# One layer's rotation angles move from VectorE to GpSimd in a two-layer hybrid block

## The chip, the cores and the metric

The kernel runs on one core of a Trainium2 chip, in one launch. The metric is the device time of that launch in microseconds (us). Engines are named as the profile names them: PE is TensorE (matmuls), DVE is VectorE, ACT is ScalarE, POOL is GpSimd, SP is SyncE (which issues the DMAs).

## The reference, cut to what matters

Two layers are applied to x (256 tokens x 1024 channels, float32). Each layer normalises x, multiplies it by one wide input matrix, feeds the columns of the product to three mixers (an attention, a gated linear attention called GLA, and a diagonal state-space scan called S5), gates and adds the three results, and ends in a feed-forward block with 4096 hidden units. The part that the change touches is the S5 mixer:

```
lam = complex(min(lam_re, -1e-4), lam_im)
step = exp(log_dt)
lam_bar = exp(lam * step)                       # 32 groups x 64 states
bu = einsum(u, b_bar)                           # complex input of each state
states = scan(s[t] = lam_bar * s[t-1] + bu[t])  # over the tokens
y = real(einsum(states, c)) + d * u
```

The kernel doesn't scan complex numbers. With lam_bar = r * exp(i * theta) it turns the input by -theta * t, scans the real and the imaginary part with the real factor r, and turns the result back. For that it needs sin and cos of theta * t for every state and every step. It works on pairs of tokens, so t runs over 128 steps, and 2048 states lie as 128 partitions x 16: two tables of 128 x 2048 per layer, `sinT` and `cosT`.

## The kernel before, in words

**Matmuls.** Each float32 product is made of three matmuls of rounded parts (lines 182 to 186, `mm3`): high x high, high x low, low x high. Weights are streamed from memory in chunks of 128 x 1024. For each chunk SP issues a DMA into `raw`, ACT rounds it to `hi` (line 164), and DVE computes `lo` = raw - hi (line 165). There are 3 `raw` buffers and 4 pairs `hi`, `lo`; a chunk is prepared 3 chunks before the one in use (`AHEAD`, lines 168 to 180). The order of the chunks is fixed when the program is built.

**Order.** The mixers of a layer are cut into steps, and the order of the steps is written out by hand in the strings `STEPS` (lines 153 to 167); a number behind a step moves its priority. A scheduler then lays out each engine's instruction list from these priorities and from what it takes to be ready. On the chip every engine works through its own list in order. An instruction whose input is late holds up everything behind it on that engine, even when that is ready.

**S5 constants.** `s5_pre` (line 319) makes the constants of the S5 mixer from the layer's parameters. It is a generator: each `P` in the first string of `STEPS` runs it to its next `yield`. For layer 0 it runs among the mixers' own steps. For layer 1 it runs during layer 0's feed-forward block (lines 1245 to 1254). It makes, in this order: the decay and the angle theta of each state (`thi` and `tlo` are the high and low part of theta / pi, lines 343 to 350); the matrices `bbar` and `cmat` (complex products on DVE in `z1` to `z4`, lines 390 to 399, spread by ACT, line 403); the transposes `Btp` of `bbar` on PE (line 438); a small matrix `K0`; then the angles.

**The angles.** Lines 456 to 474 treat four groups `ph` of 128 x 512 (four columns of states by 128 steps). For each group DVE multiplies the step number `iota` by `thi` (line 464, one instruction with both inputs broadcast), rounds to a whole turn by adding and subtracting a large constant (line 466, into the memory of `cosT`), subtracts that (line 467), adds `iota` x `tlo` (line 470, four instructions of 128 x 128), and takes off whole turns again (lines 472 and 473). ACT then makes sin, half-angle sin and its square (lines 478 to 480), and DVE turns the square into cos (line 484). The first reader of the tables is `s5_r`, lines 594 to 612, on DVE.

**POOL before.** POOL sets memory to constants (lines 270, 282, 289, 408, 409, 450, 922) and copies the decay `r2` into the scan's factor `R`, once per S5 row (line 589).

Of the kernel before, what the change touches and what calls it, by code (L numbers as in the profile page):

```python
# [14 lines left out]
ALU = mybir.AluOpType  # L15
# [71 lines left out]
class Kern:  # L87
# [231 lines left out]
    def s5_pre(self, l):  # L319
        nc, v, tt = self.nc, self.nc.vector, self.nc.vector.tensor_tensor  # L320
# [22 lines left out]
        thi = self.tiny.tile([128, n], F32R, tag="s5thi", name="thi", bufs=1)  # L343
        v.tensor_scalar(out=thi, in0=th, scalar1=1.0 / math.pi, scalar2=None, op0=ALU.mult)
        thi = thi.bitcast(F32)
        tlo = tn("tlo")
# [85 lines left out]
        for i in range(4):  # L432
# [3 lines left out]
            for q in range(4):  # L436
                c = (4 * i + q) * 128
# [6 lines left out]
        for q in range(4):  # L444
            for r in range(4):
                i = q * 4 + r
# [6 lines left out]
        s["K0"] = K0  # L453
        yield

        phs = [self.s2(f"Q{4 + i}", "ph") for i in range(4)]
        sinT, cosT = self.b8(1, "sinT"), self.b8(0, "cosT")
        kk = cosT
        for i in range(4):
            c = slice(512 * i, 512 * i + 512)  # L460
            ph = phs[i]
            ph3 = ph.rearrange("p (s c) -> p s c", s=4)
            b3 = [128, 4, 128]
            tt(out=ph3, in0=self.iota.unsqueeze(1).to_broadcast(b3),
               in1=thi[:, 4 * i:4 * i + 4].unsqueeze(2).to_broadcast(b3), op=ALU.mult)
            v.tensor_scalar(out=kk[:, c], in0=ph, scalar1=RND, scalar2=RND, op0=ALU.add, op1=ALU.subtract)
            tt(out=ph, in0=ph, in1=kk[:, c], op=ALU.subtract)
            yield
            for j in range(4):
                v.scalar_tensor_tensor(out=ph3[:, j], in0=self.iota, scalar=tlo[:, 4 * i + j:4 * i + j + 1],  # L470
                                       in1=ph3[:, j], op0=ALU.mult, op1=ALU.add)
            v.tensor_scalar(out=kk[:, c], in0=ph, scalar1=RND, scalar2=RND, op0=ALU.add, op1=ALU.subtract)
            tt(out=ph, in0=ph, in1=kk[:, c], op=ALU.subtract)
            yield
        for i in range(4):
            c = slice(512 * i, 512 * i + 512)
            ph = phs[i]
# [4 lines left out]
        for i in range(4):  # L482
            c = slice(512 * i, 512 * i + 512)
# [880 lines left out]
```

## Time and profile before

| | |
|---|---|
| median of 3 runs | 887.69 us (887.6 to 888.2) |
| the profiled execution's own time | 888.1 us |
| its span, first to last instruction | 886.3 us |
| PE busy | 866.6 us, 98% of the span |
| DVE busy | 672.6 us, 76% |
| ACT busy | 518.9 us, 59% |
| POOL busy | 22.5 us, 3% |
| granted TensorE clock, mean | 0.998 |

The span is what the trace covers; the execution's own time is 1.8 us more. Matmuls are pipelined and a matmul's end is modelled, so that a PE which is shown as busy is not proof that it lost nothing; a stretch in which PE is not shown as busy is time lost. Other engines' shares are shares of the whole span and hide that the stages differ: layer 0's mixers run from some 20 to 200 us, its feed-forward block follows.

### The profile page before, as it was taken

The numbers are of one execution on the slowest core, as the hardware profiler recorded it, in microseconds if no ns is written. First come the engines' busy times: TensorE is split into PE (matmuls) and PEld (weight loads), VectorE is DVE, ScalarE is ACT, GpSimd is POOL, SyncE is SP. The second block draws the span as 40 slices with busy tenths as digits, with TensorE's granted clock in tenths as the row PEclk, the third lists the DMA queues.
The fourth block names the chain that finished last, engine by engine and source line by source line (L and its number), as shares of the span: only waits on it lengthen the run. The fifth ranks groups of instructions, "written<-read, shape, count | busy, mean of one in ns | idle before, by whom it ended". The sixth has DMA issues, their size and how long they took to land.

```text
span 886.3 us, 16190 instructions
## 1 busy us (share of the span) xinstructions
PE 866.6 (98%) x6412; PEld 798.4 (90%) x6412; DVE 672.6 (76%) x1283; ACT 518.9 (59%) x794; POOL 22.5 (3%) x35
## 2 busy tenths in 40 slices
PE   7999999999999999999999999999999999999998
PEld 6879988899989999999988989898999899999996
DVE  7999999987767975885576887899877765555554
ACT  6877887654456565664457647874544554444441
POOL 2000000010000000000000000002000000000000
PEclk9999999999999999999999999999999999999999
DMA  7534434246664665666645644344555566656552
GB/s 259 181 122 148 153 119 145 72 153 189 190 197 159 193 192 168 190 188 190 190 143 167 184 150 150 96 143 141 170 167 167 190 187 191 185 186 184 188 190 92
DMA packets 42267, 147.79 MB, mean 167 GB/s; under 512 B 4688, under 2 KB 5328, under 8 KB 42192
## 3 DMA queue, kind: packets, MB, share of 16 engines
q1 hardware_dynamic: 42192, 146.76, 53.0%
q8 instruction: 50, 0.82, 0.4%
q14 instruction: 25, 0.20, 0.1%
HBM read 145.70 MB, written 1.05 MB: 166 GB/s over the span
## 4 chain that ended last, share of the span: by engine, by line
PE 81%; DVE 12%; ACT 3%; issue 2%; DMA 2%; SPq 0%; DVEq 0%; ACTq 0%
PE fp L184 7%; PE fp L186 7%; PE fp L185 7%; PE fo L184 7%; PE fo L185 7%; PE fo L186 7%; DVE lo L165 4%; PE gp L184 3%; PE gp L185 3%; PE gp L186 2%; PE brp L184 2%; PE brp L186 2%; PE brp L185 2%; PE wo L186 2%; PE wo L184 2%
## 5 line engine op out<-in xcount | busy, mean ns | idle before, releaser
L165 DVE TENSOR_TENSOR lo<-raw,hi 128x1024 fp32r<-128x1024 f32 (+2 forms) x276 | 332.8, 1207 | 157.7 <-ACT hi L164 156.9
L164 ACT CAST hi<-raw 128x1024 fp32r<-128x1024 f32 (+2 forms) x276 | 285.9, 1037 | 278.4 <-PE fp L185 78.9
L184 PE MATMUL fp<-h,hi 128*128 128x256 f32 x512 | 145.2, 284 | 0.0
L185 PE MATMUL fp<-h,hi 128*128 128x256 f32 x512 | 145.0, 283 | 0.0
L186 PE MATMUL fp<-h,lo 128*128 128x256 f32 x512 | 144.9, 283 | 0.0
L184 PE MATMUL gp<-h,hi 128*128 128x256 f32 x384 | 109.8, 291 | 1.0 <-ACT ppt L858 0.8
L186 PE MATMUL gp<-h,lo 128*128 128x256 f32 x384 | 107.6, 286 | 0.0
L185 PE MATMUL gp<-h,hi 128*128 128x256 f32 x384 | 107.2, 285 | 0.0
L184 PE MATMUL fo<-hi,r 128*128 128x512 f32 x256 | 100.1, 391 | 0.0
L185 PE MATMUL fo<-lo,r 128*128 128x512 f32 x256 | 99.9, 390 | 0.0
L186 PE MATMUL fo<-hi,r 128*128 128x512 f32 x256 | 99.6, 389 | 0.0
L184 PEld LDWEIGHTS fp<-h,hi 128*128 128x128 f32 x512 | 98.1, 192 | 0.9
L185 PEld LDWEIGHTS fp<-h,hi 128*128 128x128 f32 x512 | 98.2, 192 | 0.9
L186 PEld LDWEIGHTS fp<-h,lo 128*128 128x128 f32 x512 | 98.2, 192 | 0.0
L184 PEld LDWEIGHTS gp<-h,hi 128*128 128x128 f32 x384 | 72.7, 192 | 3.0 <-ACT ppt L858 1.0
L185 PEld LDWEIGHTS gp<-h,hi 128*128 128x128 f32 x384 | 72.5, 191 | 1.0 <-issue 0.5
L186 PEld LDWEIGHTS gp<-h,lo 128*128 128x128 f32 x384 | 72.6, 191 | 0.1
L186 PEld LDWEIGHTS fo<-hi,r 128*128 128x128 f32 x256 | 48.1, 188 | 10.2
L184 PEld LDWEIGHTS fo<-hi,r 128*128 128x128 f32 x256 | 48.2, 188 | 9.2
L185 PEld LDWEIGHTS fo<-lo,r 128*128 128x128 f32 x256 | 48.2, 188 | 8.9
L1054 ACT ACTIVATE gt<-gt,hgateb 128x256 f32<-128x256 f32 x48 | 21.9, 501 | 9.3 <-DVE gt L1051 9.1
L184 PE MATMUL wo<-hi,mh 128*128 128x512 f32 x64 | 24.9, 395 | 0.0
(397 smaller groups left out, 1778.5 us busy)
## 6 DMA issues: line engine op xcount, KB each, us to landing
raw<-wst SPq DMA_DIRECT2D x266, 512.0 KB, 3.6
raw<-wst SPq DMA_DIRECT2D x6, 384.0 KB, 3.2
x<-xin SPq DMA_DIRECT2D x4, 256.0 KB, 4.6
raw<-wst SPq DMA_DIRECT2D x4, 256.0 KB, 5.1
bc_raw<-bcin SPq DMA_DIRECT2D x4, 256.0 KB, 4.1
out_dram<-x SPq DMA_DIRECT2D x4, 256.0 KB, 2.0
par<-parin SPq DMA_DIRECT2D x2, 205.0 KB, 5.2
masks<-consts SPq DMA_DIRECT2D x1, 128.0 KB, 2.8
```

What stands on the lines that cost most here:

```text
L164: nc.scalar.copy(hi[:, h], raw[:, h])
L165: nc.vector.tensor_tensor(out=lo[:, h], in0=raw[:, h], in1=hi[:, h].bitcast(F32), op=ALU.subtract)
L184: mm(out, lhsT=lt[0], rhs=rt[0], start=start, stop=False)
L185: mm(out, lhsT=lt[0], rhs=rt[1], start=False, stop=False)
L186: mm(out, lhsT=lt[1], rhs=rt[0], start=False, stop=stop)
L1054: nc.scalar.activation(g[:, m, :], g[:, m, :], AF.Tanh, scale=0.5, bias=self.small[l]["gateb"][:, c:c + 1])
```

## The change

For layer 0 alone, the name `v` (and `tt`) is bound to GpSimd ahead of the loop over the groups, so every elementwise instruction after that point in `s5_pre` goes to POOL; this includes line 484 (before's number), which the diff doesn't show since its text is the same. For both layers, the one broadcast multiply of a group becomes four multiplies by a per-partition scalar, 128 x 128 each. For layer 0, the fused multiply-add with `tlo` becomes four multiplies into `kk` and one add of 128 x 512.

```diff
+        if l == 0:
+            v, tt = nc.gpsimd, nc.gpsimd.tensor_tensor
         phs = [self.s2(f"Q{4 + i}", "ph") for i in range(4)]
...
-            b3 = [128, 4, 128]
-            tt(out=ph3, in0=self.iota.unsqueeze(1).to_broadcast(b3),
-               in1=thi[:, 4 * i:4 * i + 4].unsqueeze(2).to_broadcast(b3), op=ALU.mult)
+            for j in range(4):
+                v.tensor_scalar(out=ph3[:, j], in0=self.iota, scalar1=thi[:, 4 * i + j:4 * i + j + 1], scalar2=None,
+                                op0=ALU.mult)
             v.tensor_scalar(out=kk[:, c], in0=ph, scalar1=RND, scalar2=RND, op0=ALU.add, op1=ALU.subtract)
             tt(out=ph, in0=ph, in1=kk[:, c], op=ALU.subtract)
             yield
-            for j in range(4):
-                v.scalar_tensor_tensor(out=ph3[:, j], in0=self.iota, scalar=tlo[:, 4 * i + j:4 * i + j + 1],
-                                       in1=ph3[:, j], op0=ALU.mult, op1=ALU.add)
+            if l:
+                for j in range(4):
+                    v.scalar_tensor_tensor(out=ph3[:, j], in0=self.iota, scalar=tlo[:, 4 * i + j:4 * i + j + 1],
+                                           in1=ph3[:, j], op0=ALU.mult, op1=ALU.add)
+            else:
+                for j in range(4):
+                    v.tensor_scalar(out=kk[:, 512 * i + 128 * j:512 * i + 128 * j + 128], in0=self.iota,
+                                    scalar1=tlo[:, 4 * i + j:4 * i + j + 1], scalar2=None, op0=ALU.mult)
+                tt(out=ph, in0=ph, in1=kk[:, c], op=ALU.add)
             v.tensor_scalar(out=kk[:, c], in0=ph, scalar1=RND, scalar2=RND, op0=ALU.add, op1=ALU.subtract)
             tt(out=ph, in0=ph, in1=kk[:, c], op=ALU.subtract)
             yield
```

## Rows read from the trace of the kernel before

**Rows 1.** The page: busy time by engine, and the chain that ended last.

```profile
PE 866.6 (98%) x6412; PEld 798.4 (90%) x6412; DVE 672.6 (76%) x1283; ACT 518.9 (59%) x794; POOL 22.5 (3%) x35
...
PE 81%; DVE 12%; ACT 3%; issue 2%; DMA 2%; SPq 0%; DVEq 0%; ACTq 0%
```

**Rows 2.** Busy time in stretches: PE, PEld, DVE, ACT, POOL, clock, DMA, GB/s.

```profile
30.00:46.00 16.00, 14.42 (x87) 12.08 (x85) 14.80 (x49) 14.85 (x22) 0.72 (x2) 1.00 0.54 165
...
56.00:70.00 14.00, 14.00 (x184) 12.22 (x183) 14.00 (x36) 9.96 (x19) 0.00 (x0) 1.00 0.37 119
70.00:86.00 16.00, 16.00 (x110) 14.78 (x109) 14.78 (x46) 12.28 (x19) 0.00 (x0) 1.00 0.48 147
86.00:98.00 12.00, 12.00 (x77) 11.12 (x76) 11.11 (x47) 7.85 (x11) 0.00 (x0) 1.00 0.54 168
...
110.00:122.00 12.00, 11.41 (x107) 10.69 (x106) 10.77 (x33) 11.85 (x20) 0.00 (x0) 1.00 0.24 75
122.00:134.00 12.00, 10.04 (x83) 9.62 (x81) 11.56 (x24) 8.22 (x16) 1.55 (x2) 1.00 0.51 164
...
150.00:176.00 26.00, 25.12 (x206) 21.87 (x207) 25.92 (x59) 16.86 (x40) 0.74 (x3) 1.00 0.27 82
```

**Rows 3.** The tile `ph`, both layers: duration ns min/median/max, first and last start.

```profile
L470 DVE SCALAR_TENSOR_TENSOR ph<-con,s5tlo,ph x32: 341/346/353, 58.7 to 388.6; 128x128 f32<-128x128 f32 x32
L464 DVE TENSOR_TENSOR ph<-con,thi x8: 674/683/687, 56.3 to 383.3; 128x512 f32<-128x512 f32 x8
L466 DVE TENSOR_SCALAR cosT<-ph x8: 415/416/427, 57.3 to 385.6; 128x512 f32<-128x512 f32 x8
L467 DVE TENSOR_TENSOR ph<-ph,cosT x8: 679/682/684, 57.8 to 387.1; 128x512 f32<-128x512 f32 x8
L472 DVE TENSOR_SCALAR cosT<-ph x8: 415/420/421, 61.8 to 390.0; 128x512 f32<-128x512 f32 x8
L473 DVE TENSOR_TENSOR ph<-ph,cosT x8: 680/688/693, 63.3 to 390.4; 128x512 f32<-128x512 f32 x8
```

**Rows 4.** Groups of POOL instructions: busy us, mean ns, idle before.

```profile
L589 POOL COPY R<-s5r 128x512 f32<-128x512 f32 x8 | 10.7, 1343 | 386.8 <-DVE rot L603 255.5 <-DVE s5lbr L359 89.9 <-DVE arec L860 20.8
...
L270 POOL MEMSET ones<- 128x128 f32 x1 | 0.2, 204 | 0.3 <-POOLq L1357 0.3
```

**Rows 5.** POOL in order of time, three of the eight copies: start us, us.

```profile
34.05 0.61 POOL L589 COPY R<-s5r 128x512 f32<-128x512 f32 x1 [20.52 <-DVE s5r L334]
...
148.89 0.98 POOL L589 COPY R<-s5r 128x512 f32<-128x512 f32 x1 [20.83 <-DVE arec L860]
...
607.51 4.40 POOL L589 COPY R<-s5r 128x512 f32<-128x512 f32 x1 [18.13 <-DVE rot L603]
```

**Rows 6.** DVE in order of time beside two of those copies.

```profile
149.32 1.10 DVE L608 TENSOR_TENSOR rot<-rot,sinT 128x512 f32<-128x512 f32 x1
...
607.30 1.20 DVE L165 TENSOR_TENSOR lo<-raw,hi 128x1024 fp32r<-128x1024 f32 x1
...
610.76 0.68 DVE L610 TENSOR_TENSOR rot<-rot,cosT 128x512 f32<-128x512 f32 x1
611.36 0.68 DVE L595 TENSOR_TENSOR rot<-V,sinT 128x512 f32<-128x512 f32 x1
```

**Rows 7.** DVE in order of time, 29 to 117 us.

```profile
29.59 0.17 DVE L344 TENSOR_SCALAR thi<-s5th 128x16 fp32r<-128x16 f32 x1
...
44.19 0.41 DVE L393 TENSOR_TENSOR z<-z,z 128x256 f32<-128x256 f32 x1
...
116.47 0.68 DVE L595 TENSOR_TENSOR rot<-V,sinT 128x512 f32<-128x512 f32 x1
```

**Rows 8.** ACT, then PE, in order of time around 46 us and the first sine.

```profile
45.64 1.71 ACT L403 ACTIVATE bbar<-z 64x256 f32<-64x256 f32 x4
...
66.18 0.63 ACT L478 ACTIVATE sinT<-ph 128x512 f32<-128x512 f32 x1
...
46.58 1.71 PE L438 MATMUL Btp<-con,bbar 128*128 128x128 f32 x8 [2.16 <-issue]
```

**Rows 9.** DVE by line around 20 us: the nearest rows to the new 128x128 multiplies.

```profile
L534 DVE TENSOR_SCALAR dg<-con,nr_y 128x128 f32<-128x128 f32 x2 | 0.5, 281 | 0.0
```

**Rows 10.** Busy time of the stretch in which layer 1's angles are made.

```profile
370.00:400.00 30.00, 30.00 (x188) 27.12 (x187) 24.67 (x39) 18.65 (x24) 0.00 (x0) 1.00 0.60 181
```

## The prediction, made before the result was known

> **What bounds the kernel now.** I read the page first [rows 1]. PE is busy for 98% of the span and makes up 81% of the chain that ended last; DVE makes up 12%, POOL is busy for 3%. So the kernel as a whole waits for matmuls, and DVE can matter only where PE stands still. The second view is busy time by stretch [rows 2], which shows where that is in layer 0. From 56 to 98 us PE is busy for 14.00 of 14, 16.00 of 16 and 12.00 of 12 us: nothing is lost there, though DVE is busy for 14.00, 14.78 and 11.11. From 30 to 46 PE lacks 1.58 us, from 110 to 122 it lacks 0.59, from 122 to 134 it lacks 1.96, from 150 to 176 it lacks 0.88. In the last two stretches DVE has almost no idle time (11.56 of 12, 25.92 of 26): there DVE is the bound. The third view, order of time, places the work of the change: layer 0's angles start on DVE at 56.3 [rows 3], and the first reader of the tables starts at 116.47 [rows 7]. So the DVE work that goes away lies almost wholly in a stretch in which PE loses nothing.
>
> **What it removes.** Per group DVE does one multiply (0.683), two roundings (0.416, 0.420), two subtractions (0.682, 0.688) and four multiply-adds (4 x 0.346 = 1.384): 4.27 us by durations [rows 3], 17.1 for four groups. Line 484 goes too, four more roundings' worth, 4 x 0.42 = 1.7. That is 40 instructions and 18.8 us of busy time; instructions on DVE overlap their neighbours by some 0.08 each, so about 15.6 us of DVE's time. On the path: from 56 to 98 it is worth nothing, because matmuls cover it. What it could be worth at most is what PE lacks later, where DVE is the bound: 0.59 + 1.96 + 0.88 = 3.4 us. To get any of that, the chains behind the freed DVE time (the key norms, `k`, `u`) must come earlier and PE's list must be able to use it; PE's list is full until 110, so I take 0, with 3.4 as the other end.
>
> **What it adds on POOL.** Per group eight 128x128 multiplies, two roundings and three two-input instructions of 128x512, and four conversions of line 484 in all: 32 small ones, 12 one-input and 12 two-input large ones, 56 instructions. No row shows POOL doing arithmetic. The nearest are a one-input copy of 128x512, 0.61 us alone [rows 5], and a memset of 128x128, 0.20 [rows 4]. With 0.20, 0.61 and two copies' time (1.22) for two inputs the sum is 6.4 + 7.3 + 14.6 = 28.3 us, 7.1 a group. This is the low end. For the high end the copies' own mean is 1.343, 2.2 times the undisturbed 0.61 [rows 4, 5]: 62 us. POOL can start at 29.6 when `thi` is there [rows 7], well ahead of DVE's 56.3, since nothing else is in its list. By either end it stops at 58 to 92 us, ahead of 116.47; ACT's three steps per group (0.63 each, [rows 8] has one) fit behind it. The copies of `R`, the only POOL work behind it, are first needed after the first rotation, so they have time as well. No DMA is issued or moved.
>
> A sentence on a page: the Trainium skill, GPSIMD Engine Reference, section "Elementwise — side-by-side cycle accounting", gives 4497 ns for a two-input add of 2048 elements, from which 1.12 us for 512 would be an estimate; no run here shows it yet, and by it the low end would be 6.4 + 7.3 + 13.4 = 27.1 instead of 28.3.
>
> **The price of running beside DVE.** The copy at 607.51 took 4.40 us [rows 5]. DVE then ran five instructions back to back with two inputs in SBUF (lines 165, 608, 165, 609, 610, the first and last of them in [rows 6]), and the copy ended 0.55 after line 595 began, whose one input lies in PSUM. The copy at 148.89 took 0.98, and DVE's line 608 beside it took 1.10 us where its median is 0.683 [rows 5, 6]. So either the copy stands still, or DVE does. The Trainium skill, SBUF — State Buffer, section "Who interferes with whom", says that a DVE instruction with two SBUF inputs and a GpSimd instruction that reads SBUF exclude each other for a whole instruction and that the order of issue decides who waits; the two rows agree with the exclusion (4.40 against 0.61, 1.10 against 0.68), and by that rule taken at every turn the delay below would be its high end.
>
> Where does this hurt? Not from 56 on, where DVE is 15.6 us lighter and POOL would have to take all of that back. But between 29.6 and 56.3 nothing is removed and POOL already competes. In that stretch DVE makes the complex products for `bbar`; the last one that the first transposes need starts at 44.19 and ends at 44.60 [rows 7]; ACT spreads it at 45.64 and PE, which has stood for 2.16 us, starts `Btp` at 46.58 [rows 8]. Slack: 45.64 - 44.60 = 1.0 us. Every further microsecond by which POOL delays DVE here is a microsecond of PE. From 29.6 to 44.6 POOL can hold the inputs for 15 us at most. If it gets in only where DVE runs an instruction with one input in PSUM or stands idle, as at 607.51, I count by laying its instructions along DVE's rows a delay of about 1.5 us; if it gets a turn behind every DVE instruction, as at 148.89, about 10. Less the slack: 0.5 to 9 us. I take 2.5, nearer to the low end, because DVE's instructions here follow one another without gaps, as at 607.51.
>
> **ACT's list.** The sines stand in ACT's list where the scheduler expected the angles; it lays out POOL's instructions without knowing how often DVE will hold them up. If the angles are late, ACT stands at a sine, and behind it stand the roundings of weight chunks (line 164), the spreads and the GLA steps, for which PE waits. POOL is then alone and ends its group at its own rate, so that one wait is at most a group's 7.1 us, four are 28. The three chunks prepared ahead cover some of it. The ends are 0 (all hidden) and 28 less one wait covered, 21; I take 2.5, near the low end, because ACT has idle time from 56 to 98 (30.1 busy of 42, [rows 2]).
>
> **Layer 1.** One multiply of 0.683 becomes four of 128x128. The nearest row is 0.281 each [rows 9], 1.12 for four, the other end 0 for a gain: +0.4 us of DVE per group, 1.8 in all, at 383 to 390, where PE is busy for 30.00 of 30 and DVE for 24.67 [rows 10]. Cost nothing; uncovered it would be 1.8.
>
> **Sum.** 0 (relief) + 2.5 (products) + 2.5 (ACT's list) + 0 (layer 1) = +5.0. The profiled execution took 888.1 for a span of 886.3; the median of the runs is 887.69, 0.4 below it. On the median: 892.7.
>
> **The rivals.** (1) *Faster.* The relief counts and the contention doesn't: half to all of the 3.4 us that PE lacks from 110 to 176 comes back, 884.3 to 886.0. For it: DVE is the bound there and is free of work shortly before. Against it: PE's list is full up to 110, and the products before 46 are in POOL's way. It decides when the first group on POOL delays the products by less than the 1.0 us of slack and no sine makes ACT wait longer than the chunks ahead cover. Chance 0.21. (2) *Hidden.* POOL gets through in DVE's openings, and the relief ends in matmuls: 887.7, within 1.8 us (0.2%, about what a measurement of this kernel can tell from no change). For it: PE has no gap from 56 to 98, and what POOL takes from DVE there is first paid out of the 15.6 us that it frees. Chance 0.17. (3) *Much slower.* ACT waits at each of the four groups, about 3 to 4 us each beyond the cover: 12 to 15 us, 900 to 903. For it: the 4.40 for 0.61. Against: once PE stands, DVE stands, and POOL runs freely. Chance 0.15. The forecast, slower by 2 to 10 us: 0.47. So faster 0.21, same 0.17, slower 0.62. The range leaves out the lower half of rival 1 and most of rival 3: 885.4 to 900.0; for the likeliest case alone 889.7 to 897.7.
>
> **What would show it.** In the trace after: 56 arithmetic instructions on POOL starting near 30; POOL busy for far more than 28 us if they wait for DVE; DVE's products (lines 391 to 399) ending later than 44.6, and the wait of PE before `Btp` longer than 2.16; ACT idle before line 478 released by POOL, with PE idle behind it; DVE's total 18 us lower unless its instructions got longer. It would be wrong if the scheduler puts the sines late enough, if POOL starts behind 46 us, or if PE's gaps from 110 to 176 close. The build may also order other work differently, since DVE's load changed; that moves all lists by amounts that no row of before shows.

## The result and the profile after

The changed kernel takes 919.54 us (median of four runs, 918.87 to 919.82) against 887.64 in the runs of before beside it: ratio 1.0357, 95% interval 1.0339 to 1.0375, so 31.9 us slower. The prediction was 892.7, range 885.4 to 900.0. Its sign held; its size was a sixth of the real one. The profiled execution has a span of 917.5, 31.2 more than before's 886.3.

The page, busy time and then the chain that ended last, against [rows 1]:

```profile
PE 870.4 (95%) x6412; PEld 802.4 (87%) x6412; DVE 666.7 (73%) x1255; ACT 516.1 (56%) x793; POOL 86.9 (9%) x91
...
PE 76%; DVE 10%; POOL 7%; ACT 4%; DMA 2%; issue 1%; SPq 0%; ACTq 0%; DVEq 0%
```

POOL gained 64.4 us of busy time (22.5 before), and it now makes up 7% of the chain, where it had no part. DVE lost only 5.9 us, though 40 instructions of 18.8 us left it and 12 more short ones came in layer 1, a net 1.8 us: its other instructions took some 11 us longer. PE is busy 3.8 us longer for the same 6412 matmuls, and not busy for 47.1 us of the span against 19.7; the 27.4 more and the 3.8 make the 31.2. PE's waits from 20 to 260 us (total, times, longest):

```profile
PE Btp L438 <- POOL ph L466: 20.9, 1, 20.9
PE K0p L447 <- POOL ph L481: 7.9, 1, 7.9
```

These two make 28.8 us. Before has 2.2 at `Btp` [rows 8] and nothing listed at `K0p`, so they grew by 26.6, nearly all of the 27.4. `Btp` needs no angle: the releaser shown is only what ended last. Who keeps PE waiting shows in ACT's order of time (start, us; the bracket is the idle time before it and its releaser):

```profile
39.37 1.28 ACT L486 ACT_TABLE_LOAD   x1
59.85 0.63 ACT L486 ACTIVATE sinT<-ph 128x512 f32<-128x512 f32 x1 [19.19 <-POOL ph L481]
60.49 1.28 ACT L947 ACT_TABLE_LOAD   x1
61.79 0.63 ACT L947 ACTIVATE ep<-cs 128x512 f32<-128x512 f32 x1
62.32 1.68 ACT L403 ACTIVATE bbar<-z 64x256 f32<-64x256 f32 x4
...
89.77 0.63 ACT L486 ACTIVATE sinT<-ph 128x512 f32<-128x512 f32 x1 [8.05 <-POOL ph L481]
90.30 0.57 ACT L439 COPY Bt<-Btp 128x512 f32<-128x512 f32 x1
```

The first sine now stands in ACT's list directly behind the gates' logarithm and one weight chunk, ahead of the spreads of `bbar` (L403), on which the transposes into `Btp` depend. In before it came at 66.18, behind them [rows 8]. ACT is there at 40.66 and stands for 19.19 us at the first sine, for 8.05 at the third. The spreads start at 62.32 instead of 45.64, PE's `Btp` at 65.47 instead of 46.58. The copy of `Btp` (L439) behind the third sine ends 0.15 before PE's `K0p` starts:

```profile
65.47 1.94 PE L438 MATMUL Btp<-con,bbar 128*128 128x128 f32 x8 [20.89 <-POOL ph L466]
91.02 0.34 PE L447 MATMUL K0p<-cmat,bbar 128*32 128x32 f32 x7 [7.89 <-POOL ph L481]
```

What POOL did until the first sine could start, in order of time:

```profile
30.04 4.68 POOL L466 TENSOR_SCALAR ph<-con,thi 128x128 f32<-128x128 f32 x5 [16.42 <-DVE thi L344]
34.69 1.94 POOL L468 TENSOR_SCALAR cosT<-ph 128x512 f32<-128x512 f32 x1
36.61 1.51 POOL L466 TENSOR_SCALAR ph<-con,thi 128x128 f32<-128x128 f32 x1
38.10 1.29 POOL L469 TENSOR_TENSOR ph<-ph,cosT 128x512 f32<-128x512 f32 x1
39.37 4.52 POOL L466 TENSOR_SCALAR ph<-con,thi 128x128 f32<-128x128 f32 x3
43.87 2.19 POOL L468 TENSOR_SCALAR cosT<-ph 128x512 f32<-128x512 f32 x1
...
55.44 1.93 POOL L480 TENSOR_SCALAR cosT<-ph 128x512 f32<-128x512 f32 x1
57.34 1.25 POOL L479 TENSOR_TENSOR ph<-ph,cosT 128x512 f32<-128x512 f32 x1
58.56 1.25 POOL L481 TENSOR_TENSOR ph<-ph,cosT 128x512 f32<-128x512 f32 x1
```

The groups are mixed: by 59.81, when group 0 is done, POOL has run 26 instructions, of which one group has 13. And each is long: a rounding takes 1.93 where DVE took 0.416 [rows 3]. The windows show what it costs PE (columns as in [rows 2]; first one row of before, then the kernel after):

```profile
46.00:56.00 10.00, 9.42 (x62) 8.40 (x62) 8.07 (x12) 7.89 (x17) 0.00 (x0) 0.83 0.31 100
```

```profile
46.00:56.00 10.00, 0.00 (x0) 0.00 (x0) 3.15 (x9) 0.00 (x0) 10.00 (x13) 0.54 0.01 5
56.00:70.00 14.00, 4.53 (x19) 4.27 (x20) 4.56 (x6) 9.96 (x21) 14.00 (x12) 0.50 0.00 1
70.00:86.00 16.00, 13.12 (x119) 10.74 (x118) 9.76 (x14) 10.34 (x15) 16.00 (x15) 0.98 0.52 163
86.00:98.00 12.00, 6.99 (x97) 6.29 (x98) 3.60 (x12) 6.97 (x15) 8.05 (x10) 0.72 0.01 5
```

Between 46 and 56 PE and ACT do nothing, DMA next to nothing and DVE little; POOL alone works throughout. From 56 to 98, where PE lost nothing before [rows 2], it is busy for 24.64 of 42 us.

### The profile page after: what moved, and what is told of

It is laid out like the page before. It is cut to its first block, busy times and chain, and to the rows that moved or that the text cites. A ratio compares the mean times of both kernels' runs of the same rounds, so it can differ in the third digit from the quotient of the medians.

```text
span 917.5 us, 16214 instructions
## 1 busy us (share of the span) xinstructions
PE 870.4 (95%) x6412; PEld 802.4 (87%) x6412; DVE 666.7 (73%) x1255; ACT 516.1 (56%) x793; POOL 86.9 (9%) x91
## 4 chain that ended last, share of the span: by engine, by line
PE 76%; DVE 10%; POOL 7%; ACT 4%; DMA 2%; issue 1%; SPq 0%; ACTq 0%; DVEq 0%
PE fp L184 7%; PE fp L186 7%; PE fp L185 7%; PE fo L184 6%; PE fo L185 6%; PE fo L186 6%; PE gp L184 3%; PE gp L185 3%; PE gp L186 3%; DVE lo L165 3%; PE brp L184 2%; PE brp L186 2%; PE brp L185 2%; POOL ph L466 2%; DMA raw<-wst 2%; PE wo L186 2%
## 5 line engine op out<-in xcount | busy, mean ns | idle before, releaser
L186 PEld LDWEIGHTS fo<-hi,r 128*128 128x128 f32 x256 | 48.1, 188 | 10.2
L597 POOL COPY R<-s5r 128x512 f32<-128x512 f32 x8 | 11.9, 1486 | 331.6 <-DVE rot L611 242.6
```

Source lines behind the costliest of these rows:

```text
L186: mm(out, lhsT=lt[1], rhs=rt[0], start=False, stop=stop)
L597: nc.gpsimd.tensor_copy(R3, s["r2"][:, r].unsqueeze(2).to_broadcast([128, 4, 128]))
```

## The experiments

Three theories stand in the expectations. **Q**, the queue of ACT: ACT runs its list in order, a sine waits for POOL, and everything behind it waits too. **P**, the port: POOL's work beside DVE lengthens the work of one or both. **S**, the schedule: the build puts other work in a worse order, because DVE's load or the forms of the instructions changed. Each row of the table gives medians and the ratio to the runs of before beside it; "late" means that layer 0's sines are held back in ACT's list until the last square of the key projection.

| kernel | median us | before | ratio, 95% interval |
|---|---|---|---|
| e1 changed, sines late | 894.10 | 887.75 | 1.0062, 1.0045 to 1.0079 |
| e2 changed, sines behind the last spread | 920.38 | 887.75 | 1.0366, 1.0347 to 1.0385 |
| e3 before + idle POOL work | 898.59 | 887.75 | 1.0118, 1.0102 to 1.0133 |
| e4 split multiplies, all on DVE | 889.46 | 887.67 | 1.0019, 1.0010 to 1.0028 |
| e5 cheap forms, sines late | 904.31 | 887.70 | 1.0187, 1.0172 to 1.0202 |
| e6 as e5, POOL held | 900.20 | 887.70 | 1.0139, 1.0124 to 1.0154 |
| e8 changed, cheap forms | 909.51 | 887.70 | 1.0249, 1.0231 to 1.0266 |
| e9 before, sines late | 891.57 | 887.70 | 1.0040, 1.0026 to 1.0054 |
| e10 last group only on POOL | 906.59 | 887.67 | 1.0209, 1.0195 to 1.0223 |
| e11 as e1, POOL held | 900.19 | 887.67 | 1.0139, 1.0120 to 1.0157 |
| e12 last step only on POOL | 889.40 | 887.67 | 1.0018, 1.0009 to 1.0027 |
| e13 as e10, sines behind the last spread | 896.74 | 887.95 | 1.0098, 1.0081 to 1.0115 |
| e14 as e3, sines late | 901.67 | 887.95 | 1.0156, 1.0141 to 1.0171 |

None is faster than before.

**e1, the sines late.** The angles stay on POOL; only the place of the sines in ACT's list moves.

```diff
+            self.sin_mark = nc.scalar.activation(sqk, pk[t], AF.Square)
...
+        with (self.tc.issue_after(self.sin_mark.ins) if l == 0 else nullcontext()):
             for i in range(4):
...
                 nc.scalar.activation(sinT[:, c], ph, AF.Sin, scale=TURN)
```

> The changed kernel with one edit: in ACT's list the sines of layer 0 are held behind the last square of the key projection (some 92 us in the kernel before). Theory Q (ACT's queue: ACT stood 19.2 and 8.0 us at two sines, and PE stood 20.9 and 7.9 us for what lies behind them): both waits go, PE's loss falls to the 2 to 4 us that it also has before, time 886 to 892. Rival P (the port: POOL's reads slow DVE, and the loss passes through DVE): the sines' place changes nothing, 910 or more. Rival S (the build ordered other work worse): 900 or more.

894.10, 2 us above Q's range and well below those of P and S: 25.4 us come back, and ACT no longer waits for POOL at a sine. PE's longest wait is the one of [rows 8], longer by 1.1:

```profile
PE Btp L438 <- issue: 3.3, 1, 3.3
```

That is Q for most of the loss.

**e2, the sines behind the last spread.** The same hold, marked on the last spread instead.

```diff
-                nc.scalar.activation(out[64 * g:64 * g + 64, :, 16 * g:16 * g + 16], src[64 * g:64 * g + 64],
+                self.sin_mark = nc.scalar.activation(out[64 * g:64 * g + 64, :, 16 * g:16 * g + 16],
```

> The changed kernel with the sines held only behind the last spread of the matrices (some 49 us in the kernel before), so that the transposes no longer lie behind a sine but the weight chunks still do. Theory Q: PE's wait before the transposes falls from 20.9 to some 3 us; ACT then stands at the first sine from about 51 until POOL delivers at about 60, of which the prepared chunks cover some 5; PE loses 10 to 18 us in all, time 896 to 908: between the changed kernel and the one with the sines held to 92 us. Rival P: 915 or more, as the changed kernel.

920.38, no gain: by its number it lies in P's range, 12 us above Q's. The trace shows ACT's queue all the same. Taking the sine out of the spreads' way only moved the wait. PE's longest wait, then ACT's, in two views:

```profile
PE cp L184 <- DVE cq L245: 19.2, 1, 19.2
```

```profile
ACT sinT L487 <- POOL ph L481: 27.2, 4, 18.9
```

ACT waits 27.2 us in sum, as in the changed kernel, now at four sines, and PE another 5.9 for ACT's `kN`. What counts is when POOL delivers against when ACT arrives, not only what stands behind the first sine.

**e9, before with the sines late,** is the control for e1: DVE keeps the angles, and e1's edit is made on before.

```diff
+        with (self.tc.issue_after(self.sin_mark.ins) if l == 0 else nullcontext()):
             for i in range(4):
```

> The kernel before with only the sines held to some 92 us, angles on DVE: the price of the sines' place by itself. If the place is free, 886 to 889; if part of the 6.4 us comes from it, 890 or more.

891.57, so the late place costs 3.9 us by itself, and of e1's 6.4 us only 894.10 - 891.57 = 2.5 belong to the angles on POOL. This difference is known to a microsecond or two: e1's four runs spread over 2.4. If the two add up, ACT's queue cost 31.9 - 2.5 = 29.4 us in the changed kernel; there PE stood 27.4 longer and was busy 3.8 longer.

**e3, idle POOL work.** Before, with the 52 instructions of the angles run on POOL a second time, on a buffer that nobody reads.

```diff
+            if l == 0:
+                self.idle_a(i, thi)
             yield
+            if l == 0:
+                self.idle_b(i, tlo)
```

> The kernel before, with DVE making the angles as ever, and POOL given the 52 multiplies, roundings, subtractions and adds of the change besides, on a buffer of its own that nobody reads; the engines' lists are otherwise those of the kernel before. It shows the price of the port by itself, with no relief of DVE. Theory Q: DVE's products before 46 us end 1 to 2 us later and DVE loses some more after, time 888.5 to 894. Rival P: 900 or more.

898.59: 10.8 us with no wait on POOL's results anywhere, between the two expectations. P is real: DVE's busy time grew from 672.6 to 687.0 us for the same 1283 instructions.

```profile
PE 868.9 (97%) x6412; PEld 799.5 (89%) x6412; DVE 687.0 (77%) x1283; ACT 518.1 (58%) x794; POOL 99.7 (11%) x87
```

The price has no one place: PE's waits are 3.7 before `Btp`, 2.4 on DVE's `k` and others of 1.6 and less. Part of it may pass through ACT, which waits 6.5 us for DVE's late angles; in e14 that wait is 3.4.

**e14, the same load with the sines late,** so that ACT's list is that of e1 and only DVE's relief is missing.

> The kernel before with the sines held late (891.6) and the same POOL instructions run on an unread buffer, DVE keeping the angles: the port's price without relief, with ACT's list that of the changed kernel with late sines (894.1). P: 10.9 us as with idle POOL work and the sines in their place, so 900 to 904, and the relief of DVE is worth 6 to 10 us. Q (the price without relief was itself mostly ACT's list, kept waiting by late angles): 893 to 897, the relief worth 0 to 3 us.

901.67. As P said: against e9 POOL's load costs 10.1 us, close to e3's 10.8, and against e1 the relief of DVE is worth 7.6 under that load (in e1 POOL has the four instructions of `cosT` besides). This splits the 2.5 of e1 and e9 into +10.1 - 7.6; it doesn't measure them anew.

**e4, a new form on DVE.** Each broadcast multiply is split into four as in the change, and all of it stays on DVE. The other new form is not in it: `if True` keeps the fused multiply-adds with `tlo`, although the expectation counts their product and sum as apart.

```diff
-        if l == 0:
-            v, tt = nc.gpsimd, nc.gpsimd.tensor_tensor
...
-            if l:
+            if True:
```

> The changed kernel's forms of the angles (a multiply of 128x128 for each of 16 blocks, tlo's product and the sum apart), but all of it on DVE: no work is moved to POOL. S (it is the order in which the instructions are issued that changed): at least 900. Q (ACT's queue stands behind POOL) and P (the shared port): neither is there, so 887 to 890, DVE's own list longer by the 16 separate products and no wait of ACT on the angles over 2 us.

889.46. The first sine starts at 65.71, behind the spreads as in before, so the split multiplies don't move it; they cost 1.8 us. S falls for this form. DVE's load isn't lighter here, so e4 doesn't test that part of S; beside the sine's place, S can have no more than what e1 leaves over e9.

**e10, a quarter of the dose.** Only the last group's angles go to POOL.

```diff
+            pool = l == 0 and i >= 3
+            v = nc.gpsimd if pool else nc.vector
+            tt = v.tensor_tensor
```

> Only the last of the four groups of angles is made on POOL, a quarter of the change, and the list of ACT is left to the scheduler. Undisturbed POOL needs 8 x 0.585 + 2 x 1.93 + 3 x 1.25 = 12.3 us from about 30, so to 42.3; in the built list the first sine stands behind Ln again, where ACT arrived at 40.6 in the changed kernel. Q: ACT waits 2 to 5 us once, time 889 to 894. P: a quarter of the 10.9 us of the kernel with idle POOL work, 2.7 us: 889 to 891.5, without a wait of ACT. If POOL's two-input instructions are starved by DVE as in the kernel with cheap forms (13 us), ACT waits 10 us or more: 896 to 902.

906.59: a quarter of the work costs 18.9 us, above all three ranges. One quarter is enough to put the first sine ahead of the spreads again, behind the table load at 39.13:

```profile
49.30 0.63 ACT L492 ACTIVATE sinT<-ph 128x512 f32<-128x512 f32 x1 [8.89 <-POOL ph L487]
```

POOL's group took from 29.79 to 49.27, 19.5 us instead of my 12.3, beside a DVE that was busy for 15.95 of 16 us from 30 to 46: the four multiplies of L483 alone took 7.02. PE's wait for `Btp` became 10.6. So the cost doesn't shrink in proportion to the dose: most of it is set by where the sine stands and when the first group ends.

**e13, the quarter with the sines behind the last spread.** e10's edit with e2's hold.

> The kernel with only the last group of angles on POOL (906.6), and the sines held behind the last spread of bbar and cmat, where POOL's quarter (done at 49.2 in that run) is long finished. Q: ACT's wait of 8.9 us on POOL goes and with it PE's wait for Btp (10.6 to about 2.2), so at least 8.4 us come back: 888 to 898. P: the quarter's price lies in the POOL work itself, which stays: 903 to 907. If it comes below 887 it beats both kernels.

896.74, in Q's range: 9.9 us back, and ACT's wait of 8.9 is gone. So Q holds for the quarter as well, but 8.8 us above before remain. In the traces (894.5 against 886.3) PE stands 4.7 us longer and is busy 3.5 longer for the same matmuls. Most of the standing is at a place that e10 has too (3.7 there) and before has not. ACT, then PE, in order of time:

```profile
86.19 0.63 ACT L493 ACTIVATE sinT<-ph 128x512 f32<-128x512 f32 x1
86.84 1.28 ACT L926 ACT_TABLE_LOAD   x1
88.14 0.69 ACT L926 ACTIVATE gr<-grp,nhr 128x512 f32<-128x512 f32 x1
88.72 0.82 ACT L164 CAST hi<-raw 128x768 fp32r<-128x768 f32 x1
89.56 1.28 ACT L494 ACT_TABLE_LOAD   x1
90.86 0.63 ACT L494 ACTIVATE ph<-ph 128x512 f32<-128x512 f32 x1
91.39 0.37 ACT L705 ACTIVATE sqc<-cp 128x256 f32<-128x256 f32 x1
```

```profile
91.81 1.05 PE L711 MATMUL stp<-ones,sqc 128*128 128x1 f32 x8 [3.45 <-ACT sqc L705]
```

A sine between two `gr` costs extra table loads of 1.28 each, and PE waits 3.45 for the square behind them. Another 1.2 is at `Btp` (3.4 against 2.2). The granted clock was 0.86 from 86 to 98 and 0.89 from 134 to 150, where before had 1.00; whether that is all of the 3.5 isn't settled.

**m1, POOL's price alone.** A kernel that runs POOL's forms one after another with DVE idle, none of the block's work, and writes zeros; in place of the block stand lines such as

```diff
+        g.tensor_scalar(out=T(f"addsub512_{n}"), in0=x, scalar1=RND, scalar2=RND, op0=ALU.add, op1=ALU.subtract)
+        g.tensor_scalar(out=T(f"multadd512_{n}"), in0=x, scalar1=-2.0, scalar2=1.0, op0=ALU.mult, op1=ALU.add)
```

> Leaves out the whole computation and runs only POOL instructions, three times each, with DVE idle: rounding (add, subtract) of 128x512, multiply-add, single add, single multiply, by immediates and by a per-partition scalar, 128x512 and 128x128, two-input multiply, subtract and broadcast multiply, and a copy. From the trace of the changed kernel, where DVE stood still: 1.9 us for the rounding, 0.6 for a multiply-add of the same size, 1.25 for two inputs, 0.58 for a 128x128 multiply by a per-partition scalar. If the slow rounding comes from its pair of operations, the add-add and single-operation forms tell which; if contention made it slow, it is 0.6 here.

In order of time:

```profile
5.79 1.92 POOL L1368 TENSOR_SCALAR addsub<-x 128x512 f32<-128x512 f32 x1 [1.56 <-DMA x<-xin]
7.68 0.62 POOL L1369 TENSOR_SCALAR multadd<-x 128x512 f32<-128x512 f32 x1
8.26 1.49 POOL L1370 TENSOR_SCALAR addone<-x 128x512 f32<-128x512 f32 x1
...
11.62 1.50 POOL L1372 TENSOR_SCALAR mulone<-x 128x512 f32<-128x512 f32 x1
...
14.65 0.60 POOL L1375 TENSOR_SCALAR ptrmul<-iota,par 128x128 f32<-128x128 f32 x1
...
17.97 1.04 POOL L1382 TENSOR_TENSOR ttsub<-x 128x512 f32<-128x512 f32 x1
18.95 0.61 POOL L1383 COPY copy<-x 128x512 f32<-128x512 f32 x1
```

An add with a subtract takes three times a multiply with an add on the same tile, and a single add or a single multiply takes more than twice as long as the pair of multiply and add. So 1.93 for a rounding is POOL's own rate, not DVE's doing.

**e8, cheap forms.** POOL makes each product as one broadcast instruction and each rounding as two multiply-adds; ACT's list is left to the scheduler.

```diff
-            v.tensor_scalar(out=kk[:, c], in0=ph, scalar1=RND, scalar2=RND, op0=ALU.add, op1=ALU.subtract)
+            v.tensor_scalar(out=kk[:, c], in0=ph, scalar1=1.0, scalar2=RND, op0=ALU.mult, op1=ALU.add)
+            v.tensor_scalar(out=kk[:, c], in0=kk[:, c], scalar1=1.0, scalar2=-RND, op0=ALU.mult, op1=ALU.add)
```

> The changed kernel with POOL's work alone made shorter and ACT's list left as it is (the first sine stands at the same place): each group's multiplies by a column are one broadcast two-input multiply again, and each rounding is two multiply-adds. From the run of POOL alone a group is 4 x 1.04 + 4 x 0.62 + 1.04 = 7.7 us instead of 8 x 0.60 + 2 x 1.92 + 3 x 1.04 = 11.8, with the changed kernel's 1.25 for two inputs 8.7 instead of 12.4, so 15 to 16 us less for four. Theory Q, as it stands after the run with the sines moved to the middle (ACT waits for POOL's last group in sum, wherever its first wait lies): the wait of 27.2 us falls by these 15 to 16 and the time with it, 902 to 906. Rival P (the port): 4 to 6 us less, in proportion to the 11 us of POOL beside an unrelieved DVE: 913 to 916.

909.51, between the two. ACT's wait on POOL fell by 10.4, from 27.2 to 16.8, and the time by 10.0: nearly one for one. It fell by less than the 15 to 16 expected. Two broadcast products, 1.04 each in m1, took 13.27 while DVE ran without a gap (16.00 of 16 us from 30 to 46):

```profile
39.78 13.27 POOL L484 TENSOR_TENSOR cosT<-con,s5tlo 128x512 f32<-128x512 f32 x2
```

**e5, cheap forms with the sines late.** e8's and e1's edits together.

> Sines held to some 92 us and POOL's shorter forms together. What was left with the sines held alone was 6.4 us over the kernel before. If that is the port's price, it shrinks with POOL's time by about a third: 890 to 893. If it comes from the sines' place, it stays at 893 to 895.

904.31, a miss: 10.2 us worse than e1 with less work on POOL. PE waits 8.2 us for DVE's `cq`, held up by a chain of small dependent instructions (a reciprocal root). DVE in order of time, then POOL:

```profile
71.34 1.22 DVE L212 TENSOR_SCALAR gl_y<-gl_t 128x8 int32<-128x8 int32 x1
72.59 1.21 DVE L215 TENSOR_TENSOR gl_t<-gl_y 128x8 f32<-128x8 f32 x1
...
79.45 0.55 DVE L216 SCALAR_TENSOR_TENSOR gl_t<-gl_t,glms 128x8 f32<-128x8 f32 x1
```

```profile
71.25 2.54 POOL L477 TENSOR_TENSOR ph<-ph,cosT 128x512 f32<-128x512 f32 x2
...
79.35 1.21 POOL L467 TENSOR_SCALAR cosT<-cosT 128x512 f32<-128x512 f32 x2
```

An instruction that takes 0.16 in before takes 1.22 beside POOL's two-input ones (2.54 for two) and 0.55 beside its multiply-adds (1.21 for two). That is as if it waited out a whole POOL instruction and POOL then had the next turn. In e1 the same chain runs beside a slow rounding; DVE, then POOL:

```profile
70.18 0.58 DVE L217 SCALAR_TENSOR_TENSOR gl_y<-gl_t,gl_y 128x8 f32<-128x8 f32 x1
70.80 0.17 DVE L215 TENSOR_TENSOR gl_t<-gl_y 128x8 f32<-128x8 f32 x1
71.00 0.17 DVE L216 SCALAR_TENSOR_TENSOR gl_t<-gl_t,glms 128x8 f32<-128x8 f32 x1
```

```profile
70.13 1.93 POOL L468 TENSOR_SCALAR cosT<-ph 128x512 f32<-128x512 f32 x1
```

The one that begins with POOL's takes 0.58; those behind it, while the same POOL instruction still runs, take 0.17. POOL's fast forms hold DVE up where its slow one does so only at its start.

**e6, e5 with POOL held** behind DVE's last product for `bbar`, by a small POOL copy that reads it; the angles are issued behind that copy.

```diff
+        if l == 0:
+            hold = nc.gpsimd.tensor_copy(self.ty("s5hold", n, bufs=1), D1i[:, :, 0])
...
+            with (self.tc.issue_after(hold.ins) if l == 0 else nullcontext()):
```

> As the one before, and POOL's angles are held behind the last complex product of DVE (a copy of 16 columns of it stands ahead of them in POOL's list), so that POOL doesn't compete before about 48 us. Theory: PE's wait before the transposes goes back to the 2.2 us of the kernel before, and DVE is relieved where POOL competes: 887 to 891. If the early stretch is not where the rest is lost, no better than without the hold. It is the candidate for a version that beats both.

900.20, a miss by 9. The hold did its part (PE's wait for `Btp` 6.2 in e5, 2.2 here, time 4.1 less), but the chain above still costs PE 7.9 before `cp`.

**e11, the same hold on e1.**

> As the kernel with the sines held late (894.1), and POOL's angles held behind DVE's last product for bbar as well, so that POOL starts at about 47 instead of 30 and, with 51.6 to 60 us of work, ends at 100 to 108. If the port's price falls on the products for bbar: 1 to 3 us less than the late sines alone, 891 to 893.5, and PE's wait for Btp back at 2.2. If it falls on the chain of small DVE instructions at 70 to 82, which POOL's work now covers whole: 895 to 900, with PE's cp waiting on DVE's cq.

900.19: the top of the upper range, but not for its reason. `Btp` is back at 2.2, and `cp` waits only 1.5. But POOL starts later, and the late sines catch up with it: ACT waits 8.2 us at the third sine, until 108.45, and PE 5.3 for ACT's `kT` and 3.1 for DVE's `k`. Q came back, so this run doesn't tell where the port's price falls.

**e12, the last step alone.** Only `cosT`'s four multiply-adds (line 484 of before) go to POOL.

```diff
-            v.tensor_scalar(out=cosT[:, c], in0=cosT[:, c], scalar1=-2.0, scalar2=1.0, op0=ALU.mult, op1=ALU.add)
+            (nc.vector if l else nc.gpsimd).tensor_scalar(out=cosT[:, c], in0=cosT[:, c], scalar1=-2.0, scalar2=1.0, op0=ALU.mult, op1=ALU.add)
```

> The kernel before with only the last step of the rotation (four multiply-adds on cosT, 0.62 us each on POOL) moved to POOL, behind the sines. Q: nothing on ACT waits for it, so 887 to 888.5. P: 2.5 us of POOL work beside DVE costs at most a twentieth of 10.9, 0.5 us: 887 to 888.5 as well. S: the lists of ACT change in 83 lines only, so no more than 1 us either way.

889.40: 1.7 us slower, just above the expected 888.5. Even this last step gains nothing; whether 1.7 is the port or the changed lists wasn't tried.

## Why the prediction missed

**What bounds the kernel** held in the main: of the 31.2 us, 27.4 are time in which PE stands. The other 3.8 are PE's busy time, longer for the same matmuls, which the prediction didn't count.

**"ACT's list" is the step that failed,** with +2.5 taken and 21 as its other end. The mechanism was named, ACT standing at a sine with the spreads behind it. Its bound, "one wait is at most a group's 7.1 us", was wrong. The first wait was 19.19, the two 27.2, and PE's two waits behind them grew by 26.6; e1 and e9 put the term at 29.4 if the parts add up, 26.9 above the 2.5 taken, as much as the forecast fell short (26.8). That four waits of 7.1 also make 28 is chance. Three things made it so. First, the sine moved: I read its place from before (66.18), but in the kernel after its table load starts at 39.37, ahead of the spreads; e10 does the same with a quarter on POOL, e4 doesn't with none. That the scheduler counts on an early POOL is the likely reason; no run shows its reckoning. Second, POOL mixes the groups: 26 instructions lay before the first sine, not 13. Third, they are slow: by m1's rates the 26 need 18 x 0.60 + 3 x 1.92 + 5 x 1.04 = 21.8 us, three times my 7.1; they took 29.8. The cover that I counted, ACT's idle time from 56 to 98, was no cover: the spreads stood behind the first sine until 62.32, however idle ACT was later. Wait and price go together: ACT's first wait of 0, 8.9, 15.7 and 19.2 (e1, e10, e8, the changed kernel) stands beside PE's wait for `Btp` of 3.3, 10.6, 20.4 and 20.9.

**"What it adds on POOL"** was mis-sized at its low end: 28.3 against 32 x 0.60 + 8 x 1.92 + 12 x 1.04 + 4 x 0.62 = 49.5 alone and 64.1 in the kernel; the high end, 62, was near. The bounds from a memset (0.20) and a copy (0.61) failed for one-input arithmetic, 0.60 and 1.92; two copies' time for two inputs, 1.22, was close to 1.04. The Trainium skill, GPSIMD Engine Reference, section "Elementwise — side-by-side cycle accounting", states 4497 ns for a two-input add of 2048 elements; the estimate of 1.12 for 512 from it lies near m1's 1.04.

**"The price of running beside DVE"** was right in kind where I looked: the products came 1.8 us later (L393 at 45.95, before 44.19 [rows 7]), and in e1 PE's wait for `Btp` grew by 1.1, inside the stated 0.5 to 9 and under half of the 2.5 taken. From 56 on I set POOL's load against the relief and counted neither; e3 and e14 put the whole load, without relief, at 10 to 11 us.

**"What it removes", worth 0,** is worth 7.6 us under POOL's load, by e14 against e1; alone it wasn't measured. That load and relief come to the 2.5 that the prediction took for the products is luck: of e1's 2.5, only 1.1 shows at `Btp`.

**Layer 1 at 0** stands as a reading: its angles run from 382 to 424, and PE is busy for 30.00 of 30 us from 370 to 400, as in [rows 10], and again from 400 to 430. The new multiplies take 0.280 each, as estimated.

**The rivals.** "Much slower" had the mechanism at the wrong size (3 to 4 us at each of four groups; it was 19 and 8 at two). "Faster" asked that the products come at most 1.0 us later and that no sine keep ACT waiting beyond the cover; they came 1.8 later, and ACT waited 27.2. "Hidden" rested on PE having no gap from 56 to 98, which the moved sine broke. What stays open: where the port's 10 us fall, what the relief is worth alone, how much of PE's 3.8 longer busy time the clock below explains, and part of e13's 8.8.

## What to carry to other kernels

When work moves to an emptier engine, ask first where the scheduler will now put its consumers. Here they moved ahead of work that PE needed, and one consumer too early in an in-order queue cost nearly the full lateness of its producer. Price the new engine by a run of the exact operation pairs, not by a copy or a memset. Moving work between DVE and POOL trades relief (7.6 us here) against their contention (10.1), and cheaper POOL instructions can be the worse neighbours.

## What the runs showed of the hardware that was not expected

- **POOL's rate depends on the pair of operations.** For 128x512, 0.62 us for multiply-add against 1.92 for add-subtract, both with constants, and 1.49 and 1.50 for a single add and a single multiply (m1).
- **Turn about between DVE and POOL.** Small DVE instructions of 0.16 took 0.54 to 1.22, about the length of one POOL instruction each (e5), and POOL's two products took 13.27 beside a gapless DVE (e8). The Trainium skill, SBUF — State Buffer, section "Who interferes with whom", has a DVE instruction with two SBUF inputs contend with a GpSimd one that reads SBUF, over ports that are an exclusive lock. e5's two-input rows agree (1.21 for L215); e1's row of 0.17 for the same line in the midst of POOL's 1.93 doesn't, and the measurement decides.
- **The clock after the stand.** PE stood for 20.89 us until 65.47; in the window from 56 to 70 the granted clock was 0.50, the 1.2 GHz level, where before it was 1.00 [rows 2]. Right behind the stand a matmul of 128x512 took 0.63 us, where it takes 0.39 at the full clock. Before has the same in small: behind its wait of 2.16, the window from 46 to 56 has 0.83.
